# The weights of the first norm's vectors: half into idle q/k slots, eight pieces under way

## The chip, the cores and the metric

The kernel runs on one core of a Trainium2 chip, and its time is device time in microseconds. A run's time is that of one execution; the profile is of one execution too.

## What is computed

Two layers of a transformer over 512 tokens of width 1024. The vector `c` gives shifts and scales for the norms of each layer; the first layer's attention is a differential attention, the second's has three branches, and both layers end in a mixture of 32 experts. The part around the change is the first lines of layer 0:

```python
c_act = jax.nn.silu(c)
mod = c_act @ ada_w[i] + ada_b[i]
sh1, sc1, g1, sh2, sc2, g2 = jnp.split(mod[:, None, :], 6, axis=-1)
h = _rmsnorm(x, norm_g[i, 0]) * (1.0 + sc1) + sh1
...
q, k, v = jnp.split(h @ w_in, 3, axis=-1)
```

The shift `sh1` and the scale `sc1` of layer 0 need 2048 of the 6144 columns of `ada_w[0]`: 1024 x 2048 numbers of 4 bytes, 8 MB.

## The kernel before

**Staging.** Weights pass through SBUF in pieces of 512 KB, all issued by SP. They land in a ring of two units of 128 x 4096 numbers (`unit()`, four pieces each), or in eight slots (`slot(i)`) of 128 x 2048. The slots 0 and 1 hold the transposed rows of x (`xT`) at first, and the slots 0 to 5 are later q and k of the projection units (`qs, kh, kl`); for the first unit these are written only when its sums are evacuated. Slots 2 to 5 hold nothing before that.

**Pacing.** `piece` (L111) gives each weight transfer a wait for the one `paced` transfers before it: three as a rule (`DEPTH_Q`), eight (`DEPTH_X`) for the bulk of the experts' weights. Loads of x (L453) and the small loads that ScalarE issues are not paced.

**Counters.** Beside these waits, each transfer of SP and of ScalarE's queue raises one of eight completion counters, `DMAHW0` to `DMAHW7` in the rows of the order. They are dealt out in program order, round and round over both queues, and a transfer that gets a counter that another transfer raised before waits until that one has landed.

**The opening.** `ada_first` (L193) loads two small columns and runs `ada_steps` (L179) for block 0 of layer 0: eight steps over the contraction; each step needs two pieces (1024 columns each) and makes four products into one bank. The 16 pieces fill the ring's units twice, so the second half (pieces 9 to 16) waits until the products have read the first half. After the fourth step `x_first` (L451) is put in: four loads of x of 512 KB, each normed by its own root mean square (ScalarE squares, VectorE and GpSimd make the factor, VectorE scales), then eight groups of four transposes, one group per chunk k of the contraction; ScalarE and VectorE copy the groups out in turn (`copy_any`). When all products are done, ScalarE copies the sums (`ada_raw`, L204), 32 records of small products turn them into columns (L209), and VectorE makes the scale `A` and the shift `sh` (L214 to L216).

**Other loads at that time.** ScalarE issues three broadcasts for the next vectors early (`ada_block`, L225 and L228): twice 256 KB of `ada_b` and once 128 KB of `norm_g`, each a few rows of DRAM repeated 32 times; then `lam_b` (128 KB) and `subg` (64 KB). Nothing in the opening reads the three broadcasts.

**The first projection.** `qk_unit(0)` (L483) loads four pieces of `diff_w_in` into ring unit 0 and calls `dense` (L338): for each chunk k, `modulate` makes `h_hi` and `h_lo` from `xT`, ScalarE and VectorE split the weights into `wh` and `wl`, and TensorE makes twelve products (four tiles of tokens, three each, L350 to L352). So the first 24 products are the chunks k = 0 and 1.

**The order** on each engine is set when the kernel is built, by a scheduler that plays the program through a timeline; on the chip each engine runs its list strictly in that order.

## Time and profile before

| what | us |
|---|---|
| median of three runs | 1419.81 |
| lowest and highest | 1417.21 and 1421.36 |
| the profiled execution | 1417.2 |
| span of its trace, first to last instruction | 1415.4 |
| TensorE busy in it | 1289.2 |

The profiled execution is 1.8 us longer than its span. In the trace, times count from the span's start. A group's idle time is put down to what ended it last. `PE` is TensorE's products, `ACT` ScalarE, `DVE` VectorE, `POOL` GpSimd; `SPq` and `ACTq` are the issues of transfers. A queue's wait is listed with the transfer that released it.

### The profile page before, as it was taken

Reading aid. Unit: us, or ns where it says so; the run is one execution under the profiler, and the core shown is the slowest. Engines: PE = TensorE matmul, PEld = TensorE weight load, DVE = VectorE, ACT = ScalarE, POOL = GpSimd, SP = SyncE. Lnnn points to the kernel's source line nnn. Section 1 sums busy time; section 2 is a strip of 40 time slices with the busy share of each in tenths; the row PEclk is TensorE's granted clock in tenths of the full one; section 3 lists DMA queues with packets and bytes.
Section 4 is the critical chain, followed back from the end, with each engine's and each line's share of the span. In section 5 each row is a group of like instructions: output and inputs, shape, how many; then the busy total and the mean of one; then the engine's idle time right before and its main releaser. Section 6 shows DMA issues by size and latency. Waiting matters only on the chain.

```text
span 1415.4 us, 18254 instructions
## 1 busy us (share of the span) xinstructions
PE 1289.2 (91%) x6431; PEld 760.4 (54%) x6431; DVE 787.2 (56%) x1791; ACT 513.0 (36%) x1188; POOL 188.4 (13%) x298
## 2 busy tenths in 40 slices
PE   4899999978879999999799799999999599999995
PEld 0687658567733544444588465556558434444342
DVE  2444756486535666655653365657635445666555
ACT  2453544454322222111453345555644222222212
POOL 0022020211110000000042211112120200000000
PEclk7999999989979999999899999999999799999998
DMA  8633673585569999992132474520063599999931
GB/s 265 218 92 129 226 236 122 185 280 194 181 240 362 389 408 407 380 346 95 52 110 90 126 251 138 139 70 1 30 183 119 167 363 376 401 409 408 363 144 60
DMA packets 104494, 309.82 MB, mean 219 GB/s; under 512 B 13776, under 2 KB 27568, under 8 KB 104388
## 3 DMA queue, kind: packets, MB, share of 16 engines
q1 hardware_dynamic: 93920, 288.59, 57.4%
q0 software_dynamic: 6240, 12.95, 2.7%
q10 hardware_dynamic: 4228, 6.96, 1.6%
q8 instruction: 55, 0.90, 0.3%
q14 instruction: 51, 0.42, 0.1%
HBM read 310.51 MB, written 6.33 MB: 224 GB/s over the span
## 4 chain that ended last, share of the span: by engine, by line
PE 65%; DVE 6%; DMA 3%; ACT 2%; issue 1%; POOL 1%; DVEq 0%; POOLq 0%; ACTq 0%
PE b_mm L852 17%; PE b_mm L1202 5%; PE b_sc L875 4%; PE b_mm L875 4%; PE b_tr L1197 3%; PE b_sc L886 2%; PE b_tr L840 2%; PE b_mm L886 2%; DVE xs L888 2%; PE b_mm L350 2%; PE b_mm L572 2%; PE b_mm L573 2%; PE b_mm L351 2%; PE b_mm L352 2%; PE b_mm L574 2%; PE b_sc L887 2%
## 5 line engine op out<-in xcount | busy, mean ns | idle before, releaser
L852 PE MATMUL b_mm<-slot,xT 128*64 128x512 f32 x640 | 200.0, 607 | 0.0
L852 PE MATMUL b_mm<-ring,xT 128*64 128x512 f32 x384 | 135.9, 597 | 0.0
L350 PE MATMUL b_mm<-wh,h_hi 128*128 128x512 f32 (+1 forms) x320 | 116.6, 394 | 8.3 <-ACT wh L346 6.6
L351 PE MATMUL b_mm<-wl,h_hi 128*128 128x512 f32 (+1 forms) x320 | 122.1, 390 | 0.0
L352 PE MATMUL b_mm<-wh,h_lo 128*128 128x512 f32 (+1 forms) x320 | 119.9, 386 | 0.0
L845 ACT ACTIVATE xT<-b_tr,col_sh,col_A 128x128 f32<-128x128 f32 x128 | 56.4, 454 | 148.2 <-DVE xT L847 146.9
L852 PEld LDWEIGHTS b_mm<-slot,xT 128*64 128x64 f32 x640 | 58.3, 139 | 87.7 <-issue 81.7
L888 DVE TENSOR_TENSOR xs<-xs,b_sc 128x512 f32<-128x512 f32 x128 | 83.1, 680 | 23.1 <-PE b_sc L887 23.1
L888 DVE TENSOR_TENSOR xs<-xs,b_mm 128x512 f32<-128x512 f32 x128 | 81.9, 679 | 19.3 <-PE b_mm L887 19.3
L826 POOL DMA_INDIRECT xg<-xr_d,toks x32 | 32.1, 1003 | 434.1 <-PE b_tr L840 417.5
L189 PE MATMUL b_mm<-ring,csil 128*32 128x512 f32 x384 | 79.2, 645 | 10.5 <-DMA ring<-in_ada_w_dram 5.6
L855 ACT ACTIVATE sl<-b_mm 128x256 f32<-128x256 f32 x32 | 12.3, 384 | 187.7 <-PE b_mm L852 187.7
L857 DVE TENSOR_TENSOR ac<-b_mm,sl 128x256 f32<-128x256 f32 x32 | 19.8, 618 | 108.4 <-ACT sl L855 108.4
L347 DVE TENSOR_TENSOR wl<-ring,wh 128x512 fp32r<-128x512 f32 (+1 forms) x80 | 53.6, 679 | 38.3 <-ACT wh L346 37.6
L374 DVE TENSOR_REDUCE nm<-b_sc 128x1 f32<-128x128 f32 (+3 forms) x116 | 54.4, 482 | 32.2 <-PE b_sc L369 31.2
L350 PEld LDWEIGHTS b_mm<-wh,h_hi 128*128 128x128 f32 x320 | 60.5, 192 | 20.1 <-ACT wh L346 7.5
L1199 ACT ACTIVATE pT<-b_tr 128x512 f32<-128x512 f32 x80 | 47.3, 597 | 62.6 <-PE b_tr L1197 62.2
L358 ACT ACTIVATE yh<-y 128x512 fp32r<-128x512 f32 x64 | 39.9, 632 | 79.4 <-DVE y L878 79.4
L352 PEld LDWEIGHTS b_mm<-wh,h_lo 128*128 128x128 f32 x320 | 60.7, 190 | 11.0
L351 PEld LDWEIGHTS b_mm<-wl,h_hi 128*128 128x128 f32 x320 | 60.6, 190 | 10.9
L852 PEld LDWEIGHTS b_mm<-ring,xT 128*64 128x64 f32 x384 | 39.9, 137 | 49.4 <-issue 46.7
L346 ACT ACTIVATE wh<-ring 128x512 fp32r<-128x512 f32 (+1 forms) x80 | 48.4, 614 | 46.3 <-PE b_mm L352 38.0
(327 smaller groups left out, 2683.5 us busy)
## 6 DMA issues: line engine op xcount, KB each, us to landing
ring<-in_ada_w_dram SPq DMA_DIRECT2D x96, 512.0 KB
slot<-in_moe_w_gate_dram SPq DMA_DIRECT2D x80, 512.0 KB
slot<-in_moe_w_up_dram SPq DMA_DIRECT2D x80, 512.0 KB
dn<-in_moe_w_down_dram SPq DMA_DIRECT2D x80, 512.0 KB
slot<-in_moe_w_down_dram SPq DMA_DIRECT2D x48, 512.0 KB
ring<-in_moe_w_gate_dram SPq DMA_DIRECT2D x48, 512.0 KB
ring<-in_moe_w_up_dram SPq DMA_DIRECT2D x48, 512.0 KB
ring<-in_diff_w_in_dram SPq DMA_DIRECT2D x24, 512.0 KB
```

Of the source, the lines that this page charges most:

```text
L189: mm(acc[32 * g:32 * g + 32, :], lhsT, w[:, c0:c0 + 512], start=(k == 0), stop=(k == KC - 1), skip_group_check=True)
L347: nc.vector.tensor_tensor(wl[:, :n], w[:, k, :], wh[:, :n].bitcast(F32), op=OP.subtract)
L350: mm(accs[t][:, :n], hi[:, k, tt], wh[:, :n], start=(k == 0), stop=False)
L351: mm(accs[t][:, :n], hi[:, k, tt], wl[:, :n], start=False, stop=False)
L352: mm(accs[t][:, :n], lo[:, k, tt], wh[:, :n], start=False, stop=(k == KC - 1))
L374: nc.vector.tensor_reduce(nm, b[:, :n], axis=AX.X, op=OP.max, negate=True)
L845: nc.scalar.activation(xT[:, k, :], src, AF.Identity, scale=g.Ac[:, k:k + 1], bias=g.shc[:, k:k + 1])
L852: mm(hb[64 * a:64 * a + 64, :].rearrange("p (z n) -> p z n", z=2), xT[:, k, 64 * a:64 * a + 64], gu(a, k), start=(k == 0), stop=(k == KC - ...
L875: mm(yb[64 * a:64 * a + 64, :], aT[:, k, 64 * a:64 * a + 64], dn(a, k, z), start=(k == 0), stop=(k == 1), skip_group_check=True)
L886: mm(b, st[:, t * P:(t + 1) * P], yh[:, zz], start=True, stop=False)
L888: nc.vector.tensor_tensor(g.xs[:, t, zz], g.xs[:, t, zz], b, op=OP.add)
L1202: mm(ob[64 * st:64 * st + 64, :], vst[nm][:, j, 64 * gi:64 * gi + 64], pTs[st], start=(nm == "s" and j == 0), stop=False, skip_group_check ...
```

## The change

The second half of the first vectors' weights no longer reuses the ring: steps 5 and 6 load into the slots 2 and 3, steps 7 and 8 into 4 and 5 (`rooms`). All 16 pieces are paced at eight in place of three, and so are the four pieces of the first projection unit. These four come in another order: both halves (q and k columns) of chunks 1 to 4 first, then both halves of chunks 5 to 8; all units of that kind get this order, the later ones with a pace of three.

```diff
--- before.py
+++ after.py
@@ -122,7 +122,7 @@
                               reason="paced weight stream")
         stream.append(i)
 
-    def wload(dst, src):
+    def wload(dst, src, paced=DEPTH_Q):
         h = dst.shape[-1] // 2
         if len(dst.shape) == 2:
             parts = [(dst[:, 0:h], src[:, 0:h]), (dst[:, h:], src[:, h:])]
@@ -130,7 +130,7 @@
             k = dst.shape[1] // 2
             parts = [(dst[:, 0:k], src[:, 0:k]), (dst[:, k:], src[:, k:])]
         for p in parts:
-            piece(*p)
+            piece(*p, paced)
 
     def slot(i, shape, dtype=F32):
 
@@ -175,18 +175,21 @@
     nc.scalar.activation(csil, ccol, AF.Silu)
     mod_d = [[dram.tile([4, 512], F32, name=f"mod{l}_{b}") for b in range(3)] for l in range(DEPTH)]
 
-    def ada_steps(acc, l, b):
+    def ada_room():
+
+        w = unit()
+        return [w[:, kk * 2048:(kk + 1) * 2048] for kk in range(2)]
+
+    def ada_steps(acc, l, b, rooms=(), paced=DEPTH_Q):
 
         for k in range(KC):
             if k % 2 == 0:
-                w = unit()
+                ws = rooms[k // 2]() if rooms else ada_room()
                 for kk in range(2):
-                    wload(w[:, kk * 2048:(kk + 1) * 2048],
-                          ada_w[l].rearrange("(p k) n -> p k n", k=KC)[:, k + kk, b * 2048:(b + 1) * 2048])
+                    wload(ws[kk], ada_w[l].rearrange("(p k) n -> p k n", k=KC)[:, k + kk, b * 2048:(b + 1) * 2048], paced)
             lhsT = csil[:, k:k + 1].to_broadcast([P, 32])
             for g in range(4):
-                c0 = k % 2 * 2048 + g * 512
-                mm(acc[32 * g:32 * g + 32, :], lhsT, w[:, c0:c0 + 512], start=(k == 0), stop=(k == KC - 1),
+                mm(acc[32 * g:32 * g + 32, :], lhsT, ws[k % 2][:, g * 512:(g + 1) * 512], start=(k == 0), stop=(k == KC - 1),
                    skip_group_check=True)
             yield
 
@@ -197,7 +200,8 @@
         gcol = cst.tile([P, KC], F32, name="ada_gcol")
         nc.scalar.dma_start(gcol, norm_g[0, 0].rearrange("(p k) -> p k", k=KC))
         acc = bank("mm")
-        for i, _ in enumerate(ada_steps(acc, 0, 0)):
+        rooms = [ada_room] * 2 + [lambda i=i: [slot(i, [P, 2048]), slot(i + 1, [P, 2048])] for i in (2, 4)]
+        for i, _ in enumerate(ada_steps(acc, 0, 0, rooms, DEPTH_X)):
             if i == 3:
                 midway()
         raw = pool.tile([P, 512], F32, name="ada_raw", tag=tag[0], bufs=tag[1])
@@ -482,8 +486,11 @@
 
     def qk_unit(u, before=None):
         w = unit().rearrange("p (k n) -> p k n", k=KC)
-        wload(w[:, :, 0:256], w_in[:, :, u * 256:(u + 1) * 256])
-        wload(w[:, :, 256:512], w_in[:, :, D + u * 256:D + (u + 1) * 256])
+        paced = DEPTH_X if before is not None else DEPTH_Q
+        for z in (0, 4):
+            for half in range(2):
+                c0 = half * D + u * 256
+                piece(w[:, z:z + 4, half * 256:half * 256 + 256], w_in[:, z:z + 4, c0:c0 + 256], paced)
         qs, kh, kl = (slot(2 * i + u % 2, [P, 4, S], F32R) for i in range(3))
         ST[u] = (qs, kh, kl)
```

On SP's queue, these are the first transfers before. `ring_72` and `ring_73` are the two ring units, `o_n` the rows of x, and `waits` what each instruction waits for:

```order
L114 DMA ring_72<-in_ada_w_dram 128x1024 x3
L114 DMA ring_72<-in_ada_w_dram 128x1024 [waits DMAHW1_49]
L114 DMA ring_73<-in_ada_w_dram 128x1024 [waits DMAHW2_49,DVE_49,Pool_49]
L114 DMA ring_73<-in_ada_w_dram 128x1024 [waits DMAHW4_49]
L114 DMA ring_73<-in_ada_w_dram 128x1024 [waits DMAHW6_49,DMAHW5_49]
L114 DMA ring_73<-in_ada_w_dram 128x1024 [waits DMAHW1_49]
L453 DMA o_n<-in_x_dram 128x1024 [waits DMAHW0_49,DVE_49,Activation_49]
L453 DMA o_n<-in_x_dram 128x1024 [waits DMAHW2_49]
L453 DMA o_n<-in_x_dram 128x1024 [waits DMAHW3_49]
L453 DMA o_n<-in_x_dram 128x1024 [waits DMAHW4_49]
L114 DMA ring_72<-in_ada_w_dram 128x1024 [waits DMAHW5_49,PE_49]
L114 DMA ring_72<-in_ada_w_dram 128x1024 [waits DMAHW6_49,PE_49]
```

And these after, from the second piece of ring unit 1 on; `slot_263`, `slot_264`, `slot_277` and `slot_278` are slots 2 to 5:

```order
L114 DMA ring_73<-in_ada_w_dram 128x1024 [waits DMAHW2_49]
L114 DMA ring_73<-in_ada_w_dram 128x1024 [waits DMAHW4_49]
L114 DMA ring_73<-in_ada_w_dram 128x1024 [waits DMAHW6_49]
L114 DMA slot_263<-in_ada_w_dram 128x1024 [waits DMAHW7_49,DMAHW1_49]
L114 DMA slot_263<-in_ada_w_dram 128x1024 [waits DMAHW0_49]
L114 DMA slot_264<-in_ada_w_dram 128x1024 [waits DMAHW1_49]
L114 DMA slot_264<-in_ada_w_dram 128x1024 [waits DMAHW2_49]
L114 DMA slot_277<-in_ada_w_dram 128x1024 [waits DMAHW3_49]
L457 DMA o_n<-in_x_dram 128x1024 [waits DMAHW5_49,DVE_49,Activation_49]
L457 DMA o_n<-in_x_dram 128x1024 [waits DMAHW7_49]
L457 DMA o_n<-in_x_dram 128x1024 [waits DMAHW0_49]
L457 DMA o_n<-in_x_dram 128x1024 [waits DMAHW1_49]
```

The loads of x stood behind eight pieces and stand behind thirteen; the waits are for other counters now.

On ScalarE's queue, the three broadcasts, before (`bc_1104` and `bc_1674` of 256 KB, the row with 64 partitions is that of `norm_g`, 128 KB):

```order
L175 ACTIVATE csil<-ccol 128x8 [waits DMAHW0_49]
L198 DMA ada_gcol<-in_norm_g_dram 128x8
L225 DMA bc<-in_ada_b_dram 128x1x512
L225 DMA bc<-in_ada_b_dram 128x1x512 [waits DMAHW2_49]
L228 DMA bc<-in_norm_g_dram 64x1x512 [waits DMAHW3_49]
```

and after:

```order
L175 ACTIVATE csil<-ccol 128x8 [waits DMAHW0_49]
L201 DMA ada_gcol<-in_norm_g_dram 128x8
L229 DMA bc<-in_ada_b_dram 128x1x512 [waits DMAHW1_49]
L229 DMA bc<-in_ada_b_dram 128x1x512 [waits DMAHW3_49]
L232 DMA bc<-in_norm_g_dram 64x1x512 [waits DMAHW5_49]
```

Each transfer's own counter is the one that the reader of its data waits for, or that it waits for itself when it takes a used one: before, the broadcasts have counters 0, 2 and 3, which the x tiles 1, 2 and 3 take next; after, they have 1, 3 and 5, which the ada pieces 11 and 13 and x tile 1 take next.

On TensorE, the rows that end at the first projection, before (`b_tr` are transposes of x, `csil` the ada products, `b_sc` the small products):

```order
L189 MATMUL b_mm<-ring_73,csil 32x512 [waits DMAHW2_49]
L189 MATMUL b_mm<-ring_73,csil 32x512
L458 MATMUL b_tr<-ident,o_n 128x128 [waits Activation_49]
L458 MATMUL b_tr<-ident,o_n 128x128 x3
L458 MATMUL b_tr<-ident,o_n 128x128 [waits DVE_49]
L458 MATMUL b_tr<-ident,o_n 128x128 x3
L189 MATMUL b_mm<-ring_73,csil 32x512 [waits DMAHW3_49]
L189 MATMUL b_mm<-ring_73,csil 32x512
L189 MATMUL b_mm<-ring_73,csil 32x512 [waits DMAHW4_49]
L189 MATMUL b_mm<-ring_73,csil 32x512
L209 MATMUL b_sc<-ident,ada_raw 64x2 [waits Activation_49]
L209 MATMUL b_sc<-ident,ada_raw 64x2 x15
```

and after:

```order
L192 MATMUL b_mm<-slot_278,csil 32x512 [waits DMAHW4_49]
L192 MATMUL b_mm<-slot_278,csil 32x512
L462 MATMUL b_tr<-ident,o_n 128x128 [waits Activation_49]
L462 MATMUL b_tr<-ident,o_n 128x128 x3
L213 MATMUL b_sc<-ident,ada_raw 64x2 [waits Activation_49]
L213 MATMUL b_sc<-ident,ada_raw 64x2 x9
L462 MATMUL b_tr<-ident,o_n 128x128 [waits DVE_49]
L462 MATMUL b_tr<-ident,o_n 128x128 x3
L213 MATMUL b_sc<-ident,ada_raw 64x2 x6
L462 MATMUL b_tr<-ident,o_n 128x128 [waits Activation_49]
L462 MATMUL b_tr<-ident,o_n 128x128 x3
L462 MATMUL b_tr<-ident,o_n 128x128 [waits DVE_49]
```

The small products stood behind everything else; now two groups of transposes stand behind them, and one between.

## Rows read from the trace of the kernel before

**Rows 1.** The page: its span, and TensorE's busy time, share and instructions.

```profile
span 1415.4 us, 18254 instructions
...
PE 1289.2 (91%) x6431; PEld 760.4 (54%) x6431; DVE 787.2 (56%) x1791; ACT 513.0 (36%) x1188; POOL 188.4 (13%) x298
```

**Rows 2.** Busy time by stretch: the opening, at the end granted clock, DMA share, GB/s.

```profile
core 0: us, PE busy (x) PEld busy (x) DVE busy (x) ACT busy (x) POOL busy (x), PEclk, DMA share, GB/s
4.00:5.00 1.00, 0.04 (x2) 0.04 (x4) 0.00 (x0) 0.21 (x1) 0.00 (x0) 1.00 1.02 406
5.00:13.00 8.00, 5.25 (x18) 0.83 (x20) 3.96 (x28) 0.46 (x2) 0.00 (x0) 1.00 1.00 309
13.00:26.00 13.00, 6.36 (x16) 0.56 (x12) 0.58 (x2) 1.28 (x1) 0.00 (x0) 0.71 0.66 202
26.00:39.00 13.00, 8.46 (x36) 2.83 (x36) 5.18 (x13) 5.78 (x11) 2.20 (x4) 0.64 0.97 345
19.40:22.70 3.30, 2.08 (x6) 0.19 (x4) 0.00 (x0) 0.00 (x0) 0.00 (x0) 0.64 0.25 91
```

**Rows 3.** What SP's queue waited for until 51 us: total, times, longest.

```profile
SPq L114 <- DMA ring<-in_ada_w_dram: 21.6, 13, 4.3
...
SPq L453 <- DMA bc<-in_ada_b_dram: 9.4, 2, 6.2
...
SPq L453 <- DMA bc<-in_norm_g_dram: 2.0, 1, 2.0
```

**Rows 4.** SP's issues in order of time: start, duration, line, transfer.

```profile
0.73 0.39 SPq L114 DMA_DIRECT2D ring<-in_ada_w_dram  x1
...
4.51 0.33 SPq L114 DMA_DIRECT2D ring<-in_ada_w_dram  x1
...
16.16 0.33 SPq L453 DMA_DIRECT2D o_n<-in_x_dram  x1
...
22.74 0.33 SPq L453 DMA_DIRECT2D o_n<-in_x_dram  x1
...
25.04 0.80 SPq L453 DMA_DIRECT2D o_n<-in_x_dram  x2
```

**Rows 5.** The same view of ScalarE and VectorE: x tile 4, and the first copy.

```profile
30.32 1.06 ACT L314 ACTIVATE junk<-o_n 128x1024 bf16<-128x1024 f32 x1
...
32.56 0.75 DVE L321 TENSOR_SCALAR o_n<-o_n,r_h 128x1024 f32<-128x1024 f32 x1 [0.66 <-POOL r_h L316]
...
34.88 0.60 ACT L382 ACTIVATE slot<-b_tr 128x512 f32<-128x512 f32 x1 [3.41 <-PE b_tr L458]
```

**Rows 6.** The same view of TensorE, 32 to 47 us.

```profile
32.52 1.92 PE L189 MATMUL b_mm<-ring,csil 128*32 128x512 f32 x4
...
40.24 1.05 PE L189 MATMUL b_mm<-ring,csil 128*32 128x512 f32 x4
...
41.22 1.16 PE L458 MATMUL b_tr<-ident,o_n 128*128 128x128 f32 x8
...
42.31 1.64 PE L189 MATMUL b_mm<-ring,csil 128*32 128x512 f32 x8
...
44.65 2.09 PE L209 MATMUL b_sc<-ident,ada_raw 128*64 128x2 f32 x32 [0.70 <-ACT ada_raw L204]
```

**Rows 7.** ScalarE, then TensorE, at the start of the first projection.

```profile
47.25 2.94 ACT L334 ACTIVATE h_hi<-slot,col_sh,col_A 128x512 fp32r<-128x512 f32 x4 [2.65 <-DVE col_A L215]
...
50.09 0.61 ACT L346 ACTIVATE wh<-ring 128x512 fp32r<-128x512 f32 x1
...
50.75 2.07 PE L350 MATMUL b_mm<-wh,h_hi 128*128 128x512 f32 x4 [4.02 <-ACT wh L346]
...
58.78 0.39 PE L350 MATMUL b_mm<-wh,h_hi 128*128 128x512 f32 x1
```

**Rows 8.** Busy time by stretch, columns as in the second group: the first projection.

```profile
50.75:55.60 4.85, 4.85 (x11) 3.80 (x12) 2.77 (x5) 3.67 (x6) 0.00 (x0) 0.50 0.91 304
60.00:70.00 10.00, 10.00 (x46) 8.29 (x45) 5.12 (x8) 4.49 (x8) 0.00 (x0) 1.00 0.32 103
```


## Prediction

> **What bounds the kernel now.** I read the shares first: TensorE is busy for 1289.2 of 1415.4 us [rows 1], so a microsecond is saved where TensorE waits, and the change touches only the opening, up to the first projection. There I read the transfers by stretch [rows 2], then what SP's queue waits for [rows 3], its issues [rows 4], and last the chain from the data to the first projection on the engines [rows 5 to 7].
>
> The reader is to see that the opening waits for data, and that the data wait for something odd. 406 GB/s flow from 4 to 5 us, 309 from 5 to 13, 202 from 13 to 26, and 345 from 26 to 39 [rows 2]. The hole from 13 to 26 is no lack of ring buffers: SP stands 9.4 us in two waits for the broadcasts of ada_b and 2.0 us for that of norm_g, before loads of x that have nothing to do with them [rows 3]. The order's rows say why. Transfers of SP and ACT share eight completion counters, dealt out in turn, and a transfer that is dealt a used counter first waits for the transfer that had it. The broadcasts are slow: the first two (256 KB each) are waited for until 16.16 and 22.74 us, the third (128 KB) until 25.04 [rows 4]. While SP stood, 91 GB/s flowed at a share of 0.25 [rows 2]: about four of sixteen engines, at 23 GB/s each.
>
> Then the last ada piece feeds products that end at 43.95 [rows 6], the columns follow, and the projection starts at 50.75 [rows 7]. From there TensorE has no gap that DMA makes, so what counts is when the projection starts and how fast its first 24 products go (the 25th starts at 58.78 [rows 7]).
>
> **The change part by part.** I call the ada pieces 1 to 16 and the loads of x tiles 1 to 4.
>
> *The depth.* Eight pieces are allowed in place of three, but the counters bind first. In the new SP rows, piece 6 waits for piece 2, 7 for 3, 10 for 5: four to five are under way. Piece 11 waits for the first broadcast, 13 for the second, and x tile 1 for the third. The three waits are not removed; they move to other transfers. Where SP has work it gains a little: three under way gave 345 GB/s, 1.52 us for a piece of 524 KB; full flow is 406 GB/s, 1.29 us.
>
> *When the third broadcast lands.* Not before the 25.04 of now, I take it. Now, while the second and third are under way, SP adds two ada pieces, x tile 1 and the beginning of tile 2. After, pieces 9 to 12 can be in the same engines by then, three pieces more: 3 x 1.29 = 3.9 us if all go ahead, so 28.9; with piece 13 too, 30.2. I take 29, since the third broadcast stands behind the first two in ACT's queue and SP's pieces have the meantime.
>
> *When x lands.* Piece 1 was issued at 0.73 and landed at 4.51, when piece 4 was let go [rows 4]: 3.8 us, 1.29 of it data, so 2.5 fixed. x tile 4 lands at 29 + 2.5 + 4 x 1.29 = 36.7; now its square starts at 30.32 [rows 5]. So x is 6.4 us later than now, since thirteen ada pieces stand ahead of it in place of eight. Pieces 14 to 16 follow at 1.29: 40.5, where now the last one's products begin near 42.9 (1.64 us for eight that end at 43.95, the last four taking 1.05 [rows 6]).
>
> The bound from below needs no guess on turns: on the four shared engines, x tile 4 comes behind 17 pieces and all broadcasts. Half of the 2.5 us ahead of the data and half behind, data flow from 2.0; 17 x 1.29 = 21.9; 64 KB per engine three times at 23 GB/s = 8.4; 1.2 to land: 33.5. From above: 30.2 in place of 29, and 0.6 for lam_b and subg (192 KB at 345 GB/s), which ACT has queued there: 38.5.
>
> *Which engines.* That these are the same four each time is not in the rows. The Trainium skill (DMA: Bandwidth & Descriptors, "Why a DMA increments its semaphore by 16 and not by 1") says that a transfer's slowest dimension sets the number of engines, and that the lowest-numbered are taken: four for the first two, two of these for the third. The share of 0.25 agrees with the four; no row shows which. Were the third on other engines, 64 KB at 23 GB/s, 2.8 us, would drop out of the lower bound; with the rule the bound stands.
>
> *From x to the projection.* Now tile 4's square starts at 30.32 and it is scaled at 33.31 [rows 5]: 3.0 us, so 39.7. The new PE row order fixes what follows, and ahead of the projection stand all transposes. From the scaling: the last two transposes of the first two chunks 0.3 (0.15 each [rows 6]), a copy of 0.6 [rows 5] and 0.2 for the hand-overs, 1.1; piece 15's products 1.05; transposes of chunks 3 and 4 1.16; piece 16's products 1.05 (landed at 40.5, asked for at 43.0, so not waited for); ada_raw 0.7; 20 of the 32 small products 1.3 (2.09 for all); one transpose group 0.6; the last 12 small products 0.8; a transpose group 0.6; ACT's copy of it 0.7; then, new, the first h_hi at once 0.75, and wh 0.6. That is 10.4 us, and the projection starts at 50.1. Now four h_hi (2.94) stand ahead of wh [rows 7]; after, one: the 2.2 us saved lie in that sum. So 0.65 us are gained at the start, with -3.2 us (x at 33.5) and +1.8 us (38.5) around it.
>
> *The clock.* Now TensorE has no matmul from 46.8 to 50.75, and the projection runs to 55.6 at a granted clock of 0.50, the 1.2 GHz level [rows 8]; its first 24 products take 8.0 us. After, the transposes reach to about one to two microseconds before the start. I expect the clock up, and 24 products in 7.4. Later ones take 10.0/46 = 0.22 each [rows 8], so 5.2 for 24; but ACT now makes the second chunk's h_hi behind three others, and TensorE waits for it. Bounds: 8.0 again, or 5.2. Gain 0.6, between 0 and 2.8.
>
> *The other edits.* The slots of the second half are free until the projection is evacuated; loading into them costs no instruction. The projection's weights come in another order, both halves of chunks 1 to 4 first; they are issued right behind x and pieces 14 to 16 and land near 40.5 + 4 x 1.5 = 46.5, before wh at 49.5: nothing. If that cover went, each 1.5 us late is 1.5 us. SP's loads, ACT's table load and lam_b move by microseconds on engines that wait anyway. Behind 80 us the order has some swapped rows in the attention, one pair of experts and the second layer's projection; the work is the same and TensorE is busy: nothing, with 1 us either way.
>
> **Sum:** 0.65 + 0.6 = 1.25 us less, 1417.2 to 1415.95 in the profiled execution's own time (span 1415.4 and 1.8 around it). The median of the three runs is 1419.81, 2.6 above that execution, so 1418.6.
>
> **The rivals.** *The hole closes* (faster). If the shared engines never idle and the broadcasts come as early as now, x lands at 33.5 and the projection starts at 46.9: 3.85, and 0.6 to 2.8 from the clock: 4.4 to 6.6, about 1414.3. For it: 202 GB/s in 13 to 26 leaves room, 13 us that could carry 10 pieces and carried five. Against it: SP has to be let go by the same three landings, and each costs 2.5 us fixed. The Trainium skill's page DMA: Bandwidth & Descriptors ("Queues, rings and completion order") says that an engine takes turns between rings by whole packets; by that rule a deeper SP ring takes no more turns than a shallow one, so broadcasts would stay early. No row here shows the turns.
>
> *x is late and the clock is down* (slower). TensorE has little to do from about 30 to 39 us, while it waits for x. If it then meets its two ada groups at half clock (1.92 for four products in place of 1.05 [rows 6]: +1.7) and six transpose groups partly too (+1), with x at 38.5 (+1.8) and the projection's first products again at 8.0, the start is 50.75 - 0.65 + 1.8 + 2.7 = 54.6: 3.85 slower, and with 1 us of swapped rows 4.85, about 1424.6. It decides from x tile 4 landing after 38 with the clock down. Against it: now products and transposes of the same kind ran at the upper level from 40.24 on, after some microseconds of such work [rows 6].
>
> *The change does nothing* since the counters keep three under way wherever it matters: 1419.8. This is within the forecast's own range.
>
> **How the numbers follow.** About 0.3% (4.3 us) is what a measurement of this kernel can tell from no change. Forecast and the nothing case, all between -4.2 and +4.2: 0.69. The hole closes: 0.21. Late x with a low clock: 0.10. The chances of faster, same and slower are these. The range takes the bounds of x (-3.2 to +1.8), of the clock (0 to 2.8) and of swapped rows (1 each way), not all at their ends at once: from 1413.8, which holds most of the faster rival, to 1423.
>
> **What would show it.** Right: SP's waits in the opening still name the broadcasts, now before ada pieces and x tile 1; x tile 4's square starts between 35 and 39; the last ada product ends near 43 to 45 and the projection starts near 50; the first transposes of tile 4 come behind thirteen ada pieces; the granted clock in the first 5 us of the projection is above 0.50. Wrong: the flow from 13 to 26 us above 330 GB/s, x before 34 and the projection before 47.5 (the faster rival), or the third broadcast after 31 (the slower one). Most doubtful are the landing of the third broadcast and the clock.

## The result and the profile after

The changed kernel is slower: a median of 1429.83 us over ten runs, against 1419.28 over ten runs of the kernel before; the ratio is 1.0064 with an interval of 1.005 to 1.0078, which is 9.1 us of 1420 (the two medians alone lie 10.6 us apart, a ratio within that interval). The forecast was 1418.6, its range ended at 1423.0: it was wrong in sign and size. The profile of after has a span of 1428.8 us at a granted clock of 0.954 (before 1415.4 at 0.957).

The page of after, answering to [rows 1]:

```profile
span 1428.8 us, 18236 instructions
...
PE 1298.6 (91%) x6431; PEld 762.6 (53%) x6431; DVE 787.8 (55%) x1791; ACT 513.2 (36%) x1188; POOL 188.9 (13%) x298
```

The count of products is the same, and TensorE is busy 9.4 us longer with them. Busy time by stretch, columns as in [rows 2] and [rows 8]:

```profile
4.00:5.00 1.00, 0.23 (x2) 0.19 (x4) 0.00 (x0) 0.21 (x1) 0.00 (x0) 1.00 1.02 414
5.00:13.00 8.00, 5.80 (x20) 0.65 (x16) 3.85 (x28) 0.46 (x2) 0.00 (x0) 1.00 0.98 327
13.00:26.00 13.00, 8.83 (x20) 0.90 (x20) 0.11 (x2) 1.28 (x1) 0.00 (x0) 0.61 0.88 242
26.00:39.00 13.00, 5.20 (x12) 0.54 (x13) 1.99 (x8) 2.50 (x5) 0.55 (x1) 0.59 0.59 212
39.00:52.00 13.00, 10.88 (x52) 4.97 (x52) 3.86 (x7) 4.69 (x8) 1.65 (x3) 0.63 1.03 353
56.14:61.00 4.86, 4.01 (x16) 3.02 (x17) 3.61 (x7) 4.86 (x8) 0.00 (x0) 1.00 0.03 10
60.00:70.00 10.00, 9.99 (x44) 8.28 (x45) 7.56 (x12) 6.30 (x11) 0.00 (x0) 1.00 0.33 105
```

The hole of [rows 2] is a little less deep (242 for 202 GB/s from 13 to 26 us), but it goes on to 39 (212 for 345). What SP's queue waited for until 60 us, as in [rows 3], says why; then SP's issues, as in [rows 4], and ACT's of the broadcasts:

```profile
SPq L114 <- DMA bc<-in_ada_b_dram: 13.6, 2, 7.9
...
SPq L457 <- DMA bc<-in_norm_g_dram: 5.6, 1, 5.6
```

```profile
11.19 0.80 SPq L114 DMA_DIRECT2D slot<-in_ada_w_dram  x2
...
19.92 0.33 SPq L114 DMA_DIRECT2D slot<-in_ada_w_dram  x1
...
26.44 0.33 SPq L114 DMA_DIRECT2D slot<-in_ada_w_dram  x1
...
32.49 0.33 SPq L457 DMA_DIRECT2D o_n<-in_x_dram  x1
...
4.92 3.96 ACTq L229 DMA_DIRECT2D bc<-in_ada_b_dram  x2
...
9.73 0.54 ACTq L232 DMA_DIRECT2D bc<-in_norm_g_dram  x1
```

The waits for the broadcasts grew from 11.4 us to 19.2. They let SP go at 19.92, 26.44 and 32.49 us, where it was 16.16, 22.74 and 25.04 [rows 4]. The third was also issued later, at 9.73 where it was 7.35, since ACT's queue now stood 3.96 us at the first two and not 1.75:

```profile
5.09 1.75 ACTq L225 DMA_DIRECT2D bc<-in_ada_b_dram  x2
...
7.35 0.55 ACTq L228 DMA_DIRECT2D bc<-in_norm_g_dram  x1
```

(the last two rows are of the kernel before). The chain from x tile 4 to the first projection, ScalarE and then TensorE, as in [rows 5 to 7]:

```profile
40.89 1.06 ACT L318 ACTIVATE junk<-o_n 128x1024 bf16<-128x1024 f32 x1
...
43.04 1.92 PE L192 MATMUL b_mm<-slot,csil 128*32 128x512 f32 x4
...
45.51 1.92 PE L192 MATMUL b_mm<-slot,csil 128*32 128x512 f32 x4
47.37 1.72 PE L462 MATMUL b_tr<-ident,o_n 128*128 128x128 f32 x8
49.02 1.05 PE L192 MATMUL b_mm<-slot,csil 128*32 128x512 f32 x4
...
56.14 1.20 PE L354 MATMUL b_mm<-wh,h_hi 128*128 128x512 f32 x4 [1.46 <-ACT wh L350]
...
62.87 1.07 PE L354 MATMUL b_mm<-wh,h_hi 128*128 128x512 f32 x4
```

The projection starts at 56.14, 5.4 us later than before. Its first 24 products then take 6.7 us (to 62.87) in place of 8.0 [rows 7], at the 2.4 GHz level from the start (1.00 from 56.14 to 61 us, where [rows 8] has 0.50). So the opening costs 5.4 - 1.3 = 4.1 us. One row of POOL in the attention, in before and in after, shows the same distance far beyond the projection:

```profile
128.95 0.74 POOL L305 TENSOR_TENSOR rope_a<-qkt,rope_c 128x256 f32<-128x256 f32 x1 [40.71 <-ACT qkt L493]
```

```profile
133.06 0.74 POOL L309 TENSOR_TENSOR rope_a<-qkt,rope_c 128x256 f32<-128x256 f32 x1 [40.73 <-ACT qkt L500]
```

4.11 us. The other 5.0 of the 9.1 us come behind it.

### The profile page after: what moved, and what is told of

Read it like the earlier page. It is cut to its first block, busy times and chain, and to the rows that moved or that the text cites. A ratio compares the mean times of both kernels' runs of the same rounds, so it can differ in the third digit from the quotient of the medians.

```text
span 1428.8 us, 18236 instructions
## 1 busy us (share of the span) xinstructions
PE 1298.6 (91%) x6431; PEld 762.6 (53%) x6431; DVE 787.8 (55%) x1791; ACT 513.2 (36%) x1188; POOL 188.9 (13%) x298
## 4 chain that ended last, share of the span: by engine, by line
PE 81%; DMA 7%; DVE 7%; ACT 3%; issue 1%; POOL 1%; ACTq 0%; DVEq 0%; SPq 0%; POOLq 0%
PE b_mm L859 17%; PE b_mm L1209 5%; PE b_mm L354 5%; PE b_mm L355 5%; PE b_mm L356 5%; PE b_sc L882 4%; PE b_mm L882 4%; PE b_mm L192 4%; PE b_tr L1204 3%; PE b_sc L893 2%; PE b_tr L847 2%; PE b_mm L893 2%; DVE xs L895 2%; PE b_mm L579 2%; PE b_mm L580 2%; PE b_mm L581 2%
## 5 line engine op out<-in xcount | busy, mean ns | idle before, releaser
L192 PE MATMUL b_mm<-ring,csil 128*32 128x512 f32 x352 | 70.9, 635 | 10.4 <-DMA ring<-in_ada_w_dram 5.6
L355 PEld LDWEIGHTS b_mm<-wl,h_hi 128*128 128x128 f32 x320 | 60.6, 190 | 10.6
L859 PEld LDWEIGHTS b_mm<-ring,xT 128*64 128x64 f32 x384 | 38.8, 137 | 50.1 <-issue 48.0
```

The source lines that it names most:

```text
L192: mm(acc[32 * g:32 * g + 32, :], lhsT, ws[k % 2][:, g * 512:(g + 1) * 512], start=(k == 0), stop=(k == KC - 1), skip_group_check=True)
L355: mm(accs[t][:, :n], hi[:, k, tt], wl[:, :n], start=False, stop=False)
L859: mm(hb[64 * a:64 * a + 64, :].rearrange("p (z n) -> p z n", z=2), xT[:, k, 64 * a:64 * a + 64], gu(a, k), start=(k == 0), stop=(k == KC - ...
```

## The experiments

Two questions were put. *The opening*: do the shared completion counters hold the stream back, or the broadcasts' own traffic on a few DMA engines? *Behind it*: are the other 5 us the rows that the scheduler swaps, or something else that the change leaves?

The runs e1 and e5 are made from before, all others from after. In the table, "start" is the start of the first projection; "opening" is how much later than in before that POOL row stands, one profile each; the ratio is that of the record, from which the ratio of the medians differs by up to 0.0016 (e2); "in all" is (ratio - 1) x 1420; "behind" is their difference, uncertain by 2 to 3 us, as the ratio's interval is. "Last heads" says whether the rows of TensorE in the last two heads of the attention stand as in before or as in after; "third" are other orders, with the middle heads swapped too.

| run | start | opening | ratio (interval) | in all | behind | last heads |
|---|---|---|---|---|---|---|
| after | 56.14 | +4.1 | 1.0064 (1.005 to 1.0078) | +9.1 | +5.0 | after |
| e1 | 50.81 | +0.3 | 0.9998 (0.9981 to 1.0016) | -0.3 | -0.5 | before |
| e2 | 52.62 | +1.7 | 1.0006 (0.9986 to 1.0026) | +0.9 | -0.8 | before |
| e3 | 48.80 | -2.0 | 1.0002 (0.9985 to 1.0018) | +0.3 | +2.3 | third |
| e4 | 50.95 | -0.65 | 1.0029 (1.0013 to 1.0044) | +4.1 | +4.8 | after |
| e5 | 45.65 | -6.2 | 0.9992 (0.9974 to 1.0009) | -1.1 | +5.1 | after |
| e6 | 42.58 | -8.4 | 0.9976 (0.9958 to 0.9994) | -3.4 | +5.0 | near after |
| e7 | 55.33 | +3.7 | 1.0039 (1.0024 to 1.0054) | +5.5 | +1.8 | before |
| e8 | 54.2 | +2.15 | 1.0015 (1.0 to 1.0031) | +2.1 | -0.1 | third |
| e9 | 42.51 | -9.3 | 0.9939 (0.9918 to 0.996) | -8.7 | +0.6 | before |
| e10 | 42.5 | -9.0 | 0.9947 (0.993 to 0.9964) | -7.5 | +1.5 | before |
| e11 | 49.53 | -1.45 | 1.0044 (1.0028 to 1.0059) | +6.2 | +7.7 | after |
| e12 | 46.25 | -5.2 | 0.9986 (0.9972 to 1.0) | -2.0 | +3.2 | third |
| f1 | 45.05 | -5.4 | 1.0014 (1.0001 to 1.0027) | +2.0 | +7.4 | after |
| f2 | 54.69 | +3.5 | 1.0043 (1.0029 to 1.0057) | +6.1 | +2.6 | before |
| f3 | 46.6 | -4.8 | 1.0008 (0.9995 to 1.0021) | +1.1 | +6.0 | after |
| f4 | 46.82 | -3.9 | 1.0027 (1.0014 to 1.004) | +3.8 | +7.8 | near after |

**The broadcasts on another queue.** POOL's queue has counters of its own, so the traffic stays in the opening and the shared counters are free. Beside the counters the time of issue changes: the broadcasts leave at 1.47 to 3.15 us, where ACT's queue issued them at 5.09 to 7.35 in before and at 4.92 to 9.73 in after. Which engines they take from POOL's queue no run shows. e1 does it to the kernel before, e3 to the changed one:

```diff
-        nc.scalar.dma_start(row, bass.AP(tensor=src.tensor, offset=src.offset, ap=[[512, 4], [0, 32], [1, 512]]))
+        (nc.gpsimd if l == 0 else nc.scalar).dma_start(row, bass.AP(tensor=src.tensor, offset=src.offset, ap=[[512, 4], [0, 32], [1, 512]]))
...
-            nc.scalar.dma_start(gv[lo:lo + 64], bass.AP(tensor=src.tensor, offset=src.offset,
+            (nc.gpsimd if l == 0 else nc.scalar).dma_start(gv[lo:lo + 64], bass.AP(tensor=src.tensor, offset=src.offset,
```

> The kernel before, with one thing changed: the three slow broadcasts of the first layer's two ada blocks (ada_b twice, norm_g once) are issued by POOL's queue, whose transfers do not use the completion counters that SP and ACT share. Pace 3, places and the order of every row behind the opening stay as before; no computation is left out. Theory A (SP stands because its transfers are dealt a counter that a slow broadcast holds): SP's 9.4 + 2.0 us of waits for broadcasts are gone, the projection starts 4 to 9 us before 50.75 us, and the run is 4 to 9 us faster than before. Rival B (the broadcasts slow the stream by their traffic on the engines that they share, whoever waits): SP waits for its own pieces instead and the projection starts within 2 us of 50.75; time within 0.2% of before.

> The changed kernel, with the three slow broadcasts issued by POOL's queue, off the shared completion counters; eight pieces under way and the places of the changed kernel stay, no computation is left out; the rows of the attention stand in another order than in either kernel. Theory A: SP never waits for a broadcast, some 400 GB/s flow from 4 us on, 20 transfers of 524 KB in about 27 us: x tile 4 lands at 20 to 23 us, piece 16 at 28 to 32, projection start 38 to 42 us: 8 to 12 us before the start of the kernel before, and 12 to 16 us before that of the changed kernel (56.1). Rival B (the broadcasts' traffic on the shared engines sets the pace): the start stays at 50 to 56 us. The time also carries what the later order costs, which this run cannot separate.

In e1 SP waits for nothing but its own pieces, and yet the projection starts at 50.81, where it was 50.75, as rival B had it. What SP waited for until 52 us, and a row of e1's stretches:

```profile
SPq L114 <- DMA ring<-in_ada_w_dram: 30.9, 15, 7.1
```

```profile
13.00:26.00 13.00, 5.97 (x16) 0.74 (x16) 0.58 (x2) 0.51 (x1) 0.00 (x0) 0.99 0.90 260
```

```profile
50.81 2.07 PE L350 MATMUL b_mm<-wh,h_hi 128*128 128x512 f32 x4 [4.02 <-ACT wh L346]
```

With three under way, then, the waits on counters set nothing. In e1 the last load of x is even issued at 21.57 us where it was 25.41, and from 31.9 us on SP issues four ada pieces at the same times as in before, to 0.03 us. As I read it, pieces whose engines a broadcast uses too come late, and three late pieces stop the stream as well as a counter does. In e3, with eight under way, the same edit moves the start from 56.14 to 48.80, which lies between what the two theories expected:

```profile
48.80 2.07 PE L354 MATMUL b_mm<-wh,h_hi 128*128 128x512 f32 x4 [1.36 <-ACT wh L350]
```

There the counters cost up to 7.3 us; what part of it comes of the earlier issue isn't shown. I had named the counters for both kernels; e1 refutes that for the kernel before.

**The places, the depth and the order of the weights apart.** e2 has the new places with three under way and the old order of the projection's weights; e4 the same with the new order; e7 the new places with six under way and the old order; e8 the depth of eight and the new order with before's ring buffers. The diff is e2's; e7 has 6 as a last argument in the first line, e8 has (), DEPTH_X there, and neither e4 nor e8 has the last lines.

```diff
-        for i, _ in enumerate(ada_steps(acc, 0, 0, rooms, DEPTH_X)):
+        for i, _ in enumerate(ada_steps(acc, 0, 0, rooms)):
...
-                piece(w[:, z:z + 4, half * 256:half * 256 + 256], w_in[:, z:z + 4, c0:c0 + 256], paced)
+        wload(w[:, :, 0:256], w_in[:, :, u * 256:(u + 1) * 256])
+        wload(w[:, :, 256:512], w_in[:, :, D + u * 256:D + (u + 1) * 256])
```

> The changed kernel's places (ada pieces 9 to 16 in the idle q/k buffers), but three pieces under way everywhere and the projection's weights in the old order. Every row behind the opening stands as in the kernel before. Theory A: with three under way the counters deal the waits as before; the third broadcast lands near 25 us, x tile 4 near 30 us, and ada pieces 9 to 16 no longer wait for products: projection start 48 to 51 us, time 0 to 3 us below before. Rival (the places themselves cost: SP issues pieces ahead of what the first products need, or the rows on PE stand worse): projection start 53 to 56 us and 3 to 5 us slower than before.

> As the kernel with the new places and three under way, but the first projection's weights in the changed kernel's order. Its SP rows behind the opening and its PE rows from the third pair of heads on (row 821 of 7040) stand as in the changed kernel, not as in the kernel before. Theory C (the swapped rows behind the projection cost 5 to 9 us by themselves): projection start 48 to 51 us, yet the time is 4 to 9 us above that of the run with the weights in the old order. Rival (the later loss of the changed kernel comes from its late start or from run to run): the two are within 2 us of each other.

> The changed kernel with six ada pieces under way in place of eight and the projection's weights in the old order at three under way: x stands behind 11 ada pieces in SP's queue, and the broadcasts stay where they are. Every PE, ACT and SP row behind the opening stands as in the kernel before. Theory of two parts (the changed kernel loses 4 us in the opening, since x waits behind the ada pieces and the third broadcast, and 5 us through the swapped rows of the attention): projection start 53 to 56 us, 2 to 5 us later than before, and that distance is the same, to 0.2 us, at 333 us where the attention ends; time 2 to 5 us above before, about 5 below the changed kernel. Rival (what is lost in the attention comes from the late start): the distance grows by 5 us through the attention as in the changed kernel.

> The changed kernel without the new places: eight ada pieces allowed under way, but pieces 9 to 16 go into the ring behind the products that free it, as in the kernel before; weights of the projection in the new order. x stands behind 12 ada pieces in SP's queue. Theory (the depth moves x behind the pieces and the third broadcast, whatever the places): projection start 53 to 57 us. Rival (the places do the harm, the depth none): start 49 to 51 us. The time also holds another order of the attention's rows, which this run doesn't separate.

e2 starts at 52.62 (between its two expectations), e4 at 50.95, e7 at 55.33, e8 at 54.17. The lateness goes with the depth, with the new places or without. Behind the opening e2, e7 and e8 lose -0.8, +1.8 and -0.1, and e4, whose last heads stand as in after, +4.8. In all e4 lies 3.3 us above e2, less than the 4 to 9 of the theory and more than the 2 of the rival. Where POOL loads the router's weights (at 333.2 us in before), e7 is 3.1 us behind before and after is 9.4: in e7 the distance did not grow through the attention, though it is not the same to 0.2 us either.

**The broadcasts out of the opening.** e5 (before) and e6 (after) issue them at about 88 us, long before they are read, so neither traffic nor counter is left:

```diff
+        q = nc.gpsimd if l == 0 else nc.scalar
+        with tc.issue_after(roped[3].ins) if l == 0 else nullcontext():
+            q.dma_start(row, bass.AP(tensor=src.tensor, offset=src.offset, ap=[[512, 4], [0, 32], [1, 512]]))
```

> The kernel before, with the three broadcasts of the first layer's ada blocks issued by POOL's queue behind the last rope step of the first q/k unit (about 88 us), so that none of their traffic runs in the opening; three pieces under way, nothing left out. The attention's rows are swapped again as a result. Theory (the broadcasts' traffic, on few engines, is what slows the opening): 1.52 us a piece throughout, x tile 4 lands near 21 us, ada piece 16 near 33.5, the projection starts at 41 to 43 us (before 50.75), and the run is 4 to 10 us faster, the swapped rows taking up to 5 of it. Rival (the opening is bound by three pieces under way or by the chain from x to the projection): start at 48 to 51 us and time within 0.2% of before.

> The changed kernel with the same three broadcasts issued by POOL's queue at about 88 us; eight under way and the places stay, nothing left out. Theory: 1.29 us a piece, x tile 4 (behind 13 pieces) lands near 25 us, piece 16 near 29, the projection starts at 38.5 to 41 us, 15 to 17.5 us before that of the changed kernel; the run is 5 to 11 us faster than the kernel before, since the swapped rows take up to 5. If the depth is worth nothing without the broadcasts, the start is that of the kernel before with late broadcasts (41 to 43).

The start of the projection in e5, and the stretch and the start in e6:

```profile
45.65 2.07 PE L354 MATMUL b_mm<-wh,h_hi 128*128 128x512 f32 x4 [4.01 <-ACT wh L350]
```

```profile
13.00:26.00 13.00, 7.69 (x30) 1.00 (x28) 1.06 (x6) 2.86 (x5) 0.56 (x1) 1.00 1.03 406
```

```profile
42.58 2.07 PE L358 MATMUL b_mm<-wh,h_hi 128*128 128x512 f32 x4 [1.05 <-ACT wh L354]
```

406 GB/s where after had 242: the faster rival's stream, and more. The broadcasts cost the opening 5.1 us with three under way (50.75 to 45.65) and 13.6 with eight (56.14 to 42.58); the change is worth 3.1 us at the start only once they are gone. In the opening e5 is 6.2 us ahead of before and e6 8.4, but in all it is 1.1 and 3.4, below the 4 to 10 and 5 to 11 that were expected: 5 us are lost behind. Both starts are also later than the theory had them, by 2.7 and 1.6 us.

**The broadcasts cut.** e12 leaves them on ACT's queue, as ten transfers of 32 rows each, issued from 4.95 us on, where the first broadcast was; the last goes out at 23.46:

```diff
-        nc.scalar.dma_start(row, bass.AP(tensor=src.tensor, offset=src.offset, ap=[[512, 4], [0, 32], [1, 512]]))
+        for z in range(4):
+            nc.scalar.dma_start(row[32 * z:32 * z + 32], bass.AP(tensor=src.tensor, offset=src.offset + 512 * z, ap=[[0, 32], [1, 512]]))
```

> The changed kernel, with each of the three broadcasts cut by rows of its source into transfers of 64 KB (ten in all, 32 partitions each), still in ACT's queue. Same bytes, same elements of 2 KB. Theory (a broadcast whose slowest dimension has 4 or 2 entries runs on as many engines, at 23 GB/s each): cut so, they run on all sixteen, each holds its counter for some 3 us, SP stands for no broadcast for over 3 us, projection start 42 to 48 us. Rival (the broadcasts are slow by their elements, whatever engines): SP's waits for broadcasts add up to over 8 us again and the start stays above 52.

```profile
46.25 2.08 PE L356 MATMUL b_mm<-wh,h_hi 128*128 128x512 f32 x4 [0.84 <-ACT wh L352]
```

```profile
13.00:26.00 13.00, 7.23 (x28) 0.87 (x26) 1.51 (x9) 2.41 (x4) 0.00 (x0) 1.00 1.04 352
```

The start is 9.9 us earlier than in after, with the same bytes at 352 GB/s from 13 to 26 us, and SP waits for no broadcast. So it was their shape; whether through the traffic or through the counters that come free sooner, this run doesn't tell apart. The Trainium skill (DMA: Bandwidth & Descriptors, "Why a DMA increments its semaphore by 16 and not by 1") has it that the slowest dimension sets the number of engines: four for the old form, sixteen for 32 rows. The run's times agree (46.25 for 56.14), as did the share of 0.25 in [rows 2]; the engines themselves no row shows.

**The place of x, and both cures together.** e11 is after with ada pieces 9 to 16 held behind the loads of x; e9 adds the late broadcasts, five under way and the old order of the weights; e10 is e9 with eight and the new order. (xi is the last load of x; the first lines stand in the helper that issues a piece.)

```diff
+        if behind:
+            tc.add_manual_dep(i.ins, behind[0].ins.name,
+                              mybir.DependencyInfo(mybir.DependencyClass.NoSync, mybir.DependencyReason.DATA),
+                              reason="behind x")
...
+        behind.append(xi)
```

> The changed kernel with one edit: ada pieces 9 to 16 held behind the four loads of x in SP's queue; the broadcasts stay in ACT's queue at 5 to 10 us. Theory (the loss in the opening is that x stands behind 13 pieces and the third broadcast): only x tile 3 waits, for the first broadcast, x tile 4 lands near 25 us; pieces 9 and 11 wait for the second and third broadcast, the last piece lands at 37 to 40, projection start 46 to 50 us, 6 to 10 before the changed kernel. Rival (the last ada piece sets the start, not x): start still 53 to 56. Its rows of the attention are nearly the changed kernel's (the same from PE row 821 on), so the time is 0 to 4 us above before by the first.

> The changed kernel's places with three edits: the three broadcasts issued by POOL's queue at about 88 us, ada pieces 9 to 16 held behind the four loads of x in SP's queue, and five ada pieces under way with the projection's weights in the old order. Nothing is left out, and every PE row behind the opening stands as in the kernel before. Theory (the traffic of the broadcasts and the place of x set the opening; swapped rows set the rest): x tile 4 lands at 19 to 21 us, the last ada piece near 29, the projection starts at 37 to 41 us, 10 to 13 us before the kernel before; up to 3 us of it are lost to the clock on the way; time 7 to 12 us below before (ratio 0.9915 to 0.995). Rival (what is gained in the opening is given back behind it, whatever the order): ratio above 0.997.

> As the run with five under way, but eight, and the projection's weights in the changed kernel's order. Its rows differ from those of the kernel before only within the first value unit and head (PE rows 561 to 698 of 7040). Theory: start within 1 us of the run with five (the counters allow four to five anyway), time within 3 us of it.

e11 starts at 49.53: with the broadcasts in place, x behind thirteen pieces instead of eight cost 6.6 us. It loses it again behind (+7.7), and its time is above the 0 to 4 us that were expected. e9 starts where e6 does, but its last heads stand as in before, and it keeps what it won:

```profile
42.51 2.08 PE L364 MATMUL b_mm<-wh,h_hi 128*128 128x512 f32 x4 [1.90 <-ACT wh L360]
```

Its median is 1411.7 us, a ratio of 0.9939 (0.9918 to 0.996): faster than both kernels. Both start 1.5 us later than I expected of e9, whose time is as expected. e10 gains nearly as much (0.9947): neither five or eight under way nor the order of the weights decides.

**The rows behind the opening.** f1 to f4 were to tell the swapped rows apart, with the broadcasts late throughout: f1 has all of after's rows, f2 before's, f3 the last heads' and those of the first fetch of expert weights, f4 the last heads' and an expert pair's. Their edits are the parts above; f1 to f3 issue x behind four pieces:

```diff
-            if i == 3:
+            if i == 1:
```

> Late broadcasts, new places, x behind four ada pieces in SP's queue, eight under way, the projection's weights in the changed kernel's order. All rows behind the opening stand as in the run with x first and the broadcasts in place, that is as in the changed kernel from PE row 821 on. Opening: x tile 4 near 16 us, projection start 40 to 43 us, 8 to 10.5 before that of the kernel before. Theory C (the swapped rows cost 5 to 7 us): ratio 0.997 to 0.9995, 4 to 7 us above the run without swapped rows. Rival (they cost nothing; the others lost by chance): ratio 0.993 to 0.9955, within 2 us of it.

> As the run with all rows swapped, but three ada pieces under way and the projection's weights in the old order at eight; every PE and ACT row behind the opening stands as in the kernel before. Start 40 to 43 us. Both theories: the gain of the opening less up to 2 us, ratio 0.993 to 0.9955.

> As the run with all rows swapped, with the projection's weights in the old order at three under way: of the changed kernel's swapped rows it has those of the last heads of the attention (PE rows 1198 to 1286), the order of the first layer's first expert loads in SP's queue (rows 110 to 115) and a few within the first value unit; the expert pair and the down piece in SP's queue (rows 818 to 821) stand as before. If the heads or the first loads cost the 5 us: ratio 0.997 to 0.9995. If the expert pair does: 0.993 to 0.9955.

> Late broadcasts, new places, x behind eight ada pieces, three under way, old order of the weights at eight. Of the changed kernel's swapped rows it has those of the last heads (PE rows 1198 to 1286), of an expert pair and what follows (PE rows 2616 to 3381) and of the down piece in SP's queue (818 to 821); the first value unit and the first expert loads stand as before. Start 42 to 45 us. If the heads or the expert pair cost the 5 us: ratio 0.998 to 1.000. If the first expert loads do (rows 110 to 115): 0.994 to 0.9965.

As equal openings they are a miss: they start anywhere from 45.05 to 54.69, and all four ratios lie above every range that was expected. In f1 and f2, 137 GB/s flowed from 5 to 13 us, since SP stood at the load of x, which had to wait for VectorE to be done with that buffer; in f1:

```profile
SPq L467 <- DVE rope_c L308: 10.6, 1, 10.6
```

"Behind" can still be read: +7.4, +2.6, +6.0 and +7.8. Over all runs, the six with the last heads as in before lose -0.8 to +2.6 behind the opening (mean 0.9); the eight with after's, or nearly, +4.8 to +7.8 (mean 6.1, after among them); the three with a third order -0.1 to +3.2. f3 lacks the swapped expert pair and f4 the swapped first fetch, and both lose, so the last heads' rows are what the losing kernels have in common. That the loss goes with the order is thus shown as a grouping of seventeen kernels; that the order causes it is not.

One wait of it can be named. At the swapped expert pair, what TensorE waited for, in before (563.8 to 620 us) and in after (573.8 to 631.1 us):

```profile
PE b_tr L861 <- DVE ac L857: 2.2, 2, 1.1
```

```profile
PE b_sc L893 <- ACT yh L362: 1.6, 1, 1.6
PE b_tr L868 <- DVE ac L864: 1.6, 2, 1.1
PE b_sc L882 <- DVE aTm L387: 0.4, 1, 0.4
```

In the new order TensorE comes to the pair's last products before ScalarE has written `yh`, which they read. The stretch takes 1.3 us more in all ten kernels that swap this pair (seven of the eight, and the three with a third order), and as long as in before in the seven that don't. Most of the rest is no wait. From the POOL row to the end, before and after:

```profile
128.95:1415.40 1286.45, 1184.98 (x5941) 688.12 (x5939) 734.54 (x1660) 462.12 (x1089) 175.62 (x270) 0.96 0.63 224
```

```profile
133.06:1428.80 1295.74, 1189.94 (x5941) 691.17 (x5939) 735.35 (x1660) 462.77 (x1089) 176.26 (x270) 0.96 0.62 222
```

With the same products, TensorE is busy 5.0 us longer in after and idle 4.3 us longer. The means over the profiles, each against before's from that row on:

| | later in all | TensorE busy longer | TensorE idle longer | time at the 1.2 GHz level |
|---|---|---|---|---|
| the eight | 9.5 | 5.7 | 3.9 | 106.5 |
| the six | 3.9 | 1.2 | 2.8 | 99.1 |

So of the 5.6 us between the two groups 1.1 are idle time, as much as the expert pair accounts for, and 4.5 are busy time: the same products took longer, with a low clock for longer. In the stretch of the last heads and the router (259 to 400 us in before) the eight are 2.9 us longer than before and the six 1.1. A part lies where no row of TensorE is swapped: three of the eight (e4, e11, f1) lose 1.6 to 3.9 us between 1100 and 1191 us in before's time, none of the six more than 0.4. How the order leads to a lower clock stays open, and so does how much of this repeats: these are single profiles that scatter by several us (that of before is itself 2.1 us under its median, 1415.4 + 1.8 against 1419.28).

## Why the prediction was wrong, point by point

**The waits.** Right: the three waits stayed and moved to ada pieces and x tile 1.

**The third broadcast.** The term that was mis-sized first: 29 us, at most 30.2, measured 32.49, the sign I had named for the slower rival. I let only the landing move. But ACT's transfers are dealt from the same counters, so its issues waited too: the third left 2.4 us later, and was 5.1 us longer under way (22.8 us for 17.7). The first two landed 3.8 and 3.7 us late already. By my reading of the turns that an engine takes between rings (the Trainium skill, DMA: Bandwidth & Descriptors, "Queues, rings and completion order") they would have stayed early; on ACT's queue they did not, by these 3.8 and 3.7 us. On POOL's queue, where they leave at the same times in both, their medians from issue to landing were 17.1 us (ada_b) and 17.6 (norm_g) in e1, 15.5 and 19.4 in e3, so there the depth moved them by 2 us at most, either way.

**x tile 4.** 36.7 and at most 38.5 forecast; its square starts at 40.89. 3.5 us of the 4.2 are the broadcast; 0.7 the loads, from 32.49 to 40.89 in place of 2.5 + 4 x 1.29.

**From x to the projection.** 13.4 us forecast, 15.25 measured. The ada group at 45.51 and the eight transposes at 47.37 ran for the most part at the 1.2 GHz level (a granted clock of 0.56 from 45.5 to 49.1), 1.92 and 1.72 us where I had 1.05 and 1.16: 1.4 of the 1.85. TensorE had been busy for 5.20 of 13 us from 26 to 39, waiting for ada pieces (4.1 us) and then for x (4.4). Together 3.5 + 0.7 + 1.85 = 6.05: the forecast start of 50.1 becomes 56.14. Piece 16 was not waited for, as forecast.

**The clock in the projection.** Right in direction: up from the first product, 24 products in 6.7 us where I had 7.4 and before 8.0. It is a gain of 1.3 that the late start overlays.

**The slots and the weights' order.** Right at the start for the two together: with three under way they start at 50.95 (e4), where before has 50.75. Alone, the slots with the old order start at 52.62 (e2), and in all they cost nothing that can be told from noise (1.0006, at most 1.0026).

**The swapped rows.** Wrong: 0, with 1 us either way, on the ground that the work is the same and TensorE busy. Measured behind the opening +5.0, and 6.1 as the mean of the eight kernels with such rows, against 0.9 of the six without. That the count of products is the same says neither what each waits for in a new order, 1.3 us at the expert pair, nor at which clock it runs: TensorE's busy time itself grew by 5.0 us there.

**The cause of the hole.** I called it the counters. In before they set nothing (e1) and the broadcasts themselves cost 5.1 us (e5), by their shape as I read e12; in after the counters add up to 7.3 us (e3).

**The rivals.** "x is late and the clock is down" is what the opening did: 3.85 priced, 4.1 measured, with a start at 56.14 for 54.6 and faster first products than it had. It got 0.10, on the ground that such products had run at the upper level in before; but there x came sooner, and TensorE had idled less (busy for 8.46 us from 26 to 39). "The hole closes" needed the broadcasts cut (e12, 46.25) or gone, and then e6 started even before its 46.9, at 42.58. Where the forecast failed is in holding the landings nearly fixed while adding to the traffic against which they had to land.

## What to carry to other kernels

Before a stream is made deeper, look which transfers of other queues it shares engines and counters with: a few small ones on few engines can set its pace, as they did here, and more depth then delays them, and whatever waits for them, further. Cutting the broadcasts into transfers over all engines, or issuing them when nothing else is needed, was worth more here (9.9 and 13.6 us of the opening) than the depth. And when an edit in one place makes a scheduler move rows in another, count that as a part of the change with a price of its own: 5 of the 9 us went with it here, and most of what e5 and e6 had won; only a part of that shows as waits, so compare the busy time and the clock too.

## What the hardware showed that was not expected

The clock fell in e7 in the midst of the attention, on the same TensorE rows with the same idle time as before: three gaps of 0.37, 0.31 and 0.57 us (0.37, 0.31 and 0.58 before) close to each other. Stretches of e7, then the first of them in before, 3.7 us earlier, which is the shift between the two in the opening:

```profile
155.00:160.00 5.00, 4.00 (x19) 3.30 (x20) 4.13 (x13) 2.75 (x10) 0.00 (x0) 0.76 0.75 239
160.00:165.00 5.00, 5.00 (x23) 3.92 (x21) 3.74 (x10) 3.04 (x10) 0.00 (x0) 0.90 0.89 275
```

```profile
151.30:156.30 5.00, 4.00 (x24) 3.27 (x25) 4.96 (x15) 4.13 (x15) 0.00 (x0) 1.00 0.91 302
```

The same four products that follow took 1.98 us in e7 and 1.09 in before:

```profile
159.28 1.98 PE L354 MATMUL b_mm<-wh,h_hi 128*128 128x512 f32 x4
```

```profile
154.80 1.09 PE L350 MATMUL b_mm<-wh,h_hi 128*128 128x512 f32 x4
```

So equal rows with equal gaps do not have an equal clock. It is not e7 alone: from 25 to 30 us behind the POOL row of the table, the granted clock is 0.66 to 0.68 in seven of the eighteen profiles (after, e5, e7, e9, e10, e12, f3) and 1.00 in the other eleven. And the same broadcasts took a median of 7.5 us (ada_b) and 10.2 (norm_g) from issue to landing when they ran late in e6, and 15 to 19 in the opening on the same queue.
